# Attention outputs kept in each pattern's own order until the merge

## The chip, the cores and the metric

One Trainium2 chip, one core of it. The metric is the device time of one execution in microseconds. The profile names the engines PE (matrix multiply; PEld is its loading of weights), DVE (vector), ACT (scalar), POOL (GpSimd) and SP, whose queue issues the DMAs.

## The reference

A trunk of two layers on one sequence of 1024 tokens, width 1024: a gated mixer and an MLP, then an attention mixer and an MLP. The change concerns the attention mixer alone. It has 16 heads of 64 and three dilation patterns. Each pattern has its own queries, keys and values; a token sees only tokens of its own residue class modulo the dilation, in blocks of up to 128 with the block before. The outputs of the three patterns are weighted by a softmax over their log-sums:

```python
B_PATTERNS = ((128, 1), (512, 4), (2048, 16))

def mixer_b(h, w_qkv, w_out, slopes):
    qkv = (h @ w_qkv).reshape(B, S, N_PAT, 3, B_HEADS, B_HEAD_DIM)
    for g, (window, dilation) in enumerate(B_PATTERNS):
        o, lse = dilated_branch(qkv[:, :, g, 0], qkv[:, :, g, 1], qkv[:, :, g, 2], window, dilation, slopes)
        outs.append(o)
        lses.append(lse)
    wts = jax.nn.softmax(jnp.stack(lses, axis=0), axis=0)[..., None]
    o = jnp.sum(wts * jnp.stack(outs, axis=0), axis=0)
    return o.reshape(B, S, B_HEADS * B_HEAD_DIM).astype(h.dtype) @ w_out
```

## The kernel before, in words

All matrices are float32. A product is made of three passes, high by high, high by low and low by high part; `split` (L102 and L103) makes the two parts, the high one by a copy on ACT, the low one by a subtraction on DVE.

The attention stage works on pairs of heads, `hp` 0 to 7, and for each pair on the patterns `g` in the order 2, 1, 0: 24 groups. While the projections of later groups run on PE (`project`, L1139, with the splits of q and k and the copy of v), the softmax of the present group runs between them. The groups are cut into 8 slots of three positions, and `at(slot, pos)` puts a step into one of them: `scores` (L1212, L1213; on DVE L1219, on ACT the exponential L1221), `transposes` of the weights p (L1244, L1247, then a split into pThi and pTlo) and `weighted`, the products with v (L1267). This gives an order in the program. When the program is built, the framework's planner orders the instructions of each engine after its own model of their times, and each engine then works strictly in that order, waiting where something is not ready. The same holds for the DMAs on SP's queue.

Queries, keys and values of patterns 1 and 2 lie in the pattern's order, all tokens of one residue class side by side: in pattern 1 position `r * 256 + i` is token `4 * i + r`, in pattern 2 position `(a * 2 + b) * 64 + i` is token `16 * i + 8 * b + a`. `project` brings them into that order as it reads PSUM (`by_pos`, `perm`).

`weighted` sums the products of one head and pattern in two PSUM banks `pvs`, 512 tokens each. The high and the low part of v give two sums in the two halves of the partitions, `rest` and `main`. When both banks are full, ACT copies the one half into the tile `oT` (L1284) and DVE adds the other (L1285), 64 partitions by 512 elements each, for `b` in 0 and 1. `oT` holds both heads of the pair, 128 partitions by 1024 tokens; it is a tile of the pool `work`, tag "res", which has three buffers, one for each pattern. The residual rows of the output stage (`add_x`, L283 and L284) later use the same three buffers. In patterns 1 and 2 the destination is written in token order, so with a step of 4 or of 16 elements.

`merge` follows each pair. `statistics`, `read` and `factors` bring the sums and maxima of the three patterns through memory into token order and make the weights; `spread` reads them back, spread over 64 partitions for each head, into three tiles `bc` (`row_bc`: pool `vec`, tag "lng", three buffers; L1349). `scale` (L1352) multiplies oT by bc, pattern 1 on POOL, patterns 2 and 0 on DVE, and `add` (L1355) adds the three on DVE. For pairs 0 to 6 the sum goes to `o_dram` (L1357).

The output stage begins within the last group: `prepare` reads the sums of the pairs back into `oraw` (L1400; the first four are `row_bc` tiles, the others use the tag "raw" of the weights) and splits them into `oTs`; the last pair's sum is taken from the tile itself. `OutRows` loads the rows of the output matrix (L339, `wo_raw`), multiplies them by the gate on POOL (L344), splits them and multiplies (L356); ACT copies the first sums out (L374), DVE adds the later ones (L376).

## Time and profile before

| | |
|---|---|
| median of 3 runs | 2809.95 us (2809.93 to 2812.29) |
| profiled execution | 2810.59 us, of it the span 2808.9 us |
| attention stage | about 1040 to 2150 us |
| one pair of heads | about 133 us |

The first section of the page gives the busy time of each engine with its share of the span. In the rows of groups, the name left of the arrow is the tile written, right of it the tiles read, then the shapes, the count and the busy time with the mean of one in ns. In rows in order of time the columns are the start, the duration (both us), engine, line, operation and tiles; in brackets stands how long the engine had been idle and what ended that. In answers for one line the three numbers are the shortest, median and longest duration in ns. In rows of waits they are the sum in us, how many, and the longest.

### The profile page before, as it was taken

The numbers are of one execution on the slowest core, as the hardware profiler recorded it, in microseconds if no ns is written. First come the engines' busy times: TensorE is split into PE (matmuls) and PEld (weight loads), VectorE is DVE, ScalarE is ACT, GpSimd is POOL, SyncE is SP. The second block draws the span as 40 slices with busy tenths as digits, with TensorE's granted clock in tenths as the row PEclk, the third lists the DMA queues.
The fourth block names the chain that finished last, engine by engine and source line by source line (L and its number), as shares of the span: only waits on it lengthen the run. The fifth ranks groups of instructions, "written<-read, shape, count | busy, mean of one in ns | idle before, by whom it ended". The sixth has DMA issues, their size and how long they took to land.

```text
span 2808.9 us, 36869 instructions
## 1 busy us (share of the span) xinstructions
PE 2743.5 (98%) x13290; PEld 2279.7 (81%) x13290; DVE 1949.5 (69%) x3502; ACT 1418.3 (50%) x2625; POOL 200.7 (7%) x155
## 2 busy tenths in 40 slices
PE   6999999999999999999999999999999999999998
PEld 5787878888888878888888888888877788878887
DVE  6777798887977665556555555555659975668887
ACT  3354375555443455555555555555563755554332
POOL 1001000000000033101000000010201000000000
PEclk9999999999999999999999999999999999999999
DMA  7543347668846443212121212121215464486562
GB/s 256 159 127 105 120 152 234 214 225 280 281 152 196 133 150 111 57 47 65 37 68 39 69 32 69 39 69 38 85 47 172 164 215 150 161 285 207 168 199 93
DMA packets 300187, 384.15 MB, mean 137 GB/s; under 512 B 47533, under 2 KB 172885, under 8 KB 300005
## 3 DMA queue, kind: packets, MB, share of 16 engines
q1 hardware_dynamic: 300004, 381.80, 42.6%
q8 instruction: 104, 1.70, 0.3%
q14 instruction: 79, 0.64, 0.1%
HBM read 297.77 MB, written 83.97 MB: 136 GB/s over the span
## 4 chain that ended last, share of the span: by engine, by line
PE 77%; DVE 10%; DMA 7%; ACT 3%; issue 2%; POOL 1%; SPq 1%; DVEq 0%; POOLq 0%; ACTq 0%
PE psd L938 21%; PE psq L1139 8%; PE psv L1139 8%; PE psua L779 8%; PE psk L1139 7%; PE psuc L779 4%; PE psd_wout L356 3%; PE pv L1267 2%; DMA adaw<-in_ada_w_dram 2%; PE psu L356 2%; PE psd_wo L356 2%; PE psub L779 2%; PE psv L453 2%; PE sc L1213 1%; PE pT L1244 1%
## 5 line engine op out<-in xcount | busy, mean ns | idle before, releaser
L779 PE MATMUL psua<-right,left 128*128 128x512 f32 x1536 | 365.2, 391 | 3.3 <-ACT right L102 1.7
L938 PE MATMUL psd<-rhi,lhi 128*128 128x512 f32 x896 | 350.0, 391 | 3.0 <-ACT part L810 3.0
L938 PE MATMUL psd<-rlo,lhi 128*128 128x512 f32 x896 | 349.8, 390 | 0.2
L938 PE MATMUL psd<-rhi,llo 128*128 128x512 f32 x896 | 349.3, 390 | 0.0
L779 PEld LDWEIGHTS psua<-right,left 128*128 128x128 f32 x1536 | 287.2, 188 | 65.0 <-DVE right L103 2.9
L1221 ACT ACTIVATE p<-p,stat 128x128 f32<-128x128 f32 (+1 forms) x384 | 170.2, 444 | 231.6 <-DVE stat L1219 230.7
L1139 PE MATMUL psv<-hT,wv_hi 128*128 128x512 f32 x768 | 245.9, 401 | 2.4 <-DVE qlo L103 2.4
L1139 PE MATMUL psq<-hT,wq_hi 128*128 128x512 f32 x768 | 248.1, 404 | 0.0
L1139 PE MATMUL psk<-hT,wk_hi 128*128 128x512 f32 x768 | 247.2, 403 | 0.0
L103 DVE TENSOR_TENSOR pTlo<-pT,pThi 128x512 fp32r<-128x512 f32 (+1 forms) x160 | 98.0, 621 | 158.2 <-ACT pThi L102 157.3
L938 PEld LDWEIGHTS psd<-rhi,lhi 128*128 128x128 f32 x896 | 168.7, 188 | 38.9 <-ACT part L810 3.9
L938 PEld LDWEIGHTS psd<-rlo,lhi 128*128 128x128 f32 x896 | 168.5, 188 | 35.8 <-DVE rlo L103 1.1
L938 PEld LDWEIGHTS psd<-rhi,llo 128*128 128x128 f32 x896 | 168.7, 188 | 35.0
L779 PE MATMUL psuc<-right,left 128*128 128x512 f32 x768 | 190.5, 395 | 0.0
L128 DVE SCALAR_TENSOR_TENSOR adaacc<-adaw,silu_c,adaacc 128x512 f32<-128x512 f32 x168 | 132.7, 800 | 57.9 <-DMA adaw<-in_ada_w_dram 57.3
L779 PEld LDWEIGHTS psuc<-right,left 128*128 128x128 f32 x768 | 145.6, 191 | 30.9 <-DVE right L103 0.4
L1285 DVE TENSOR_TENSOR oT<-oT,pv 64x512 f32<-64x512 f32 x96 | 90.8, 946 | 109.3 <-ACT oT L1284 108.6
L1139 PE MATMUL psq<-hT,wq_lo 128*128 128x512 f32 x384 | 151.4, 394 | 0.0
L1139 PEld LDWEIGHTS psv<-hT,wv_hi 128*128 128x128 f32 x768 | 133.2, 189 | 22.1 <-issue 2.8
L1139 PE MATMUL psv<-hT,wv_lo 128*128 128x512 f32 x384 | 150.8, 393 | 0.0
L1139 PE MATMUL psk<-hT,wk_lo 128*128 128x512 f32 x384 | 150.6, 392 | 0.0
L1139 PEld LDWEIGHTS psk<-hT,wk_hi 128*128 128x128 f32 x768 | 133.7, 190 | 19.6
(250 smaller groups left out, 5841.2 us busy)
## 6 DMA issues: line engine op xcount, KB each, us to landing
lraw<-forms SPq DMA_DIRECT2D x112, 512.0 KB
adaw<-in_ada_w_dram SPq DMA_DIRECT2D x192, 256.0 KB
up<-in_mlp_w_up_dram SPq DMA_DIRECT2D x64, 512.0 KB
forms<-s SPq DMA_DIRECT2D x128, 256.0 KB
rraw<-in_mlp_w_down_dram SPq DMA_DIRECT2D x64, 512.0 KB
forms<-part SPq DMA_DIRECT2D x96, 256.0 KB
spill<-acc SPq DMA_DIRECT2D x24, 512.0 KB
wq_raw<-in_b_w_qkv_dram SPq DMA_DIRECT2D x24, 512.0 KB
```

Of the source, the lines that this page charges most:

```text
L103: return first, lo_engine.tensor_tensor(lo, src, hi, op=ALU.subtract)
L128: ins = V.scalar_tensor_tensor(acc[:], raw[:], silu_c[:, k : k + 1], acc[:], ALU.mult, ALU.add)
L356: T.matmul(dst, s[a], m[b], start=(n == 0), stop=(n == last))
L453: T.matmul(sums[u, half][:], units[u][a_][:, k * P : (k + 1) * P], hT[half][b_][:, k, :], start=k == 0 and a_ + b_ == 0, stop=k == KD - 1 ...
L779: T.matmul(acc, w[:, a, k, :], right[p][:, b, k, :], start=p in (1, 2, 5) and k + a + b == 0, stop=k == 3 and a == 1, skip_group_check=True)
L938: ins = T.matmul(sums[kind, m][:], l[a][:, k, m * P : (m + 1) * P], r[b][:, k, :], start=p in (1, 5, 2, 3) and kp + k + a + b == 0, stop=k ...
L1139: T.matmul(p[:], wu[a][:, k * P : (k + 1) * P], hT[half][b][:, k, :], start=k + c_ == 0, stop=k == KD - 1 and c_ == 2)
L1213: T.matmul(scb[:, sl], my["qlo"][e][:, tq], keys[:, k0 : k0 + w], start=False, stop=True)
L1221: A.activation(pr[:, 0:w], pr[:, 0:w], AF.Exp, bias=nm, scale=-1.0, accum_out=l)
L1244: T.transpose(pst[:, o : o + P], probs[t][:, P : 2 * P] if has[t] else probs[t][:, 0:P], ident[:])
L1267: T.matmul(pvs[b][:, q0 % HALF : q0 % HALF + w_], stt, x_[:, o_ : o_ + w_], start=not begun[b], stop=left[b] == 0, skip_group_check=True)
L1285: V.tensor_tensor(dst, dst, sb, op=ALU.add)
```

## The change

The sums of patterns 1 and 2 are written to oT in the pattern's own order, as those of pattern 0 always were: contiguous pieces of 512. The scale now reads oT with a step, in token order, and writes its product into the weights' tile bc, which is in token order. The adds work on the bc tiles, the store to o_dram reads the bc tile of pattern 0, and the last pair's sum is that tile. So oT is last used by its scale, and the three bc tiles are held until the adds and the store are done.

```diff
-                            if g == 0:
-                                dst = oT[rows, b * HALF : (b + 1) * HALF]
-                                sa, sb = pvs[b][rest, :], pvs[b][main, :]
-                            elif g == 1:
-                                dst = by_pos(oT[rows, :], g)[:, 2 * b : 2 * b + 2, :]
-                                sa, sb = (pvs[b][r, :].rearrange("p (r i) -> p r i", r=2) for r in (rest, main))
-                            else:
-                                dst = by_pos(oT[rows, :], g)[:, 4 * b : 4 * b + 4, :, :]
-                                sa, sb = (pvs[b][r, :].rearrange("p (a b i) -> p a b i", a=4, b=2) for r in (rest, main))
-                            A.copy(dst, sa)
-                            V.tensor_tensor(dst, dst, sb, op=ALU.add)
+                            dst = oT[rows, b * HALF : (b + 1) * HALF]
+                            A.copy(dst, pvs[b][rest, :])
+                            V.tensor_tensor(dst, dst, pvs[b][main, :], op=ALU.add)
...
                 def scale(g, engine):
-                    engine.tensor_tensor(oTs[g][:], oTs[g][:], box[g][:], op=ALU.mult)
+
+                    o, bc = oTs[g][:], box[g][:]
+                    if g == 1:
+                        o, bc = o.rearrange("p (r i) -> p i r", r=4), bc.rearrange("p (i r) -> p i r", r=4)
+                    elif g == 2:
+                        o = o.rearrange("p (a b i) -> p i b a", a=8, b=2)
+                        bc = bc.rearrange("p (i b a) -> p i b a", a=8, b=2)
+                    engine.tensor_tensor(bc, o, bc, op=ALU.mult)
 
                 def add(g):
-                    V.tensor_tensor(oTs[0][:], oTs[0][:], oTs[g][:], op=ALU.add)
-                    if g == 2 and hp < N_PAIRS - 1:
-                        nc.sync.dma_start(o_dram[hp], oTs[0][:])
+                    V.tensor_tensor(box[0][:], box[0][:], box[g][:], op=ALU.add)
+                    if g == 2:
+                        if hp < N_PAIRS - 1:
+                            nc.sync.dma_start(o_dram[hp], box[0][:])
+                        else:
+                            oTs["sum"] = box[0]
...
                     if k == N_PAIRS - 1:
-                        raw = oTs[0]
+                        raw = oTs["sum"]
```

## The prediction

> **What bounds the kernel now.** I read the page first, then the busy time by stretches, then who PE waited for in the attention stage, and last the order of time around each merge.

> ```profile
> span 2808.9 us, 36869 instructions
> ...
> PE 2743.5 (98%) x13290; PEld 2279.7 (81%) x13290; DVE 1949.5 (69%) x3502; ACT 1418.3 (50%) x2625; POOL 200.7 (7%) x155
> ...
> PE 77%; DVE 10%; DMA 7%; ACT 3%; issue 2%; POOL 1%; SPq 1%; DVEq 0%; POOLq 0%; ACTq 0%
> ```

> PE carries the span. The change touches only the attention stage, which lies between 1040 and 2150 us. Its busy times, with the columns PE, PEld, DVE, ACT, POOL, granted clock, DMA share and GB/s:

> ```profile
> core 0: us, PE busy (x) PEld busy (x) DVE busy (x) ACT busy (x) POOL busy (x), PEclk, DMA share, GB/s
> 1183.00:1316.00 133.00, 132.90 (x724) 112.93 (x723) 75.34 (x185) 72.84 (x175) 13.17 (x13) 1.00 0.20 53
> 2120.00:2142.00 22.00, 16.83 (x54) 12.13 (x55) 21.02 (x26) 4.42 (x5) 2.38 (x1) 0.84 0.69 224
> ```

> One pair of heads takes 133 us. In it PE is busy 132.90 us and DVE and ACT a little over half. Work taken from DVE or ACT there is worth nothing unless PE waits for exactly that work. Behind the last pair the picture is turned round: DVE is busy 21.02 of 22 us and PE only 16.83. There DVE sets the pace. What PE waited for in the two places:

> ```profile
> PEld pT L1244 <- ACT p L1221: 5.1, 13, 1.1
> PE psd_wo L356 <- DVE acc L376: 3.8, 2, 2.0
> ```

> So all waits of PE's loads for the softmax weights sum to 5.1 us in the whole stage, and they stand mostly at the merges, which the change edits. The third merge, in order of time:

> ```profile
> 1452.15 2.40 POOL L1352 TENSOR_TENSOR oT<-oT,bc 128x1024 f32<-128x1024 f32 x1 [1.73 <-DMA bc<-w_dram]
> 1454.29 1.35 DVE L1352 TENSOR_TENSOR oT<-oT,bc 128x1024 f32<-128x1024 f32 x1 [0.55 <-DMA bc<-w_dram]
> 1456.61 0.29 DVE L1219 CUSTOM_DVE_ANT_0 p<-sc,bias 128x128 f32<-128x128 f32 x1
> 1457.18 0.39 ACT L1221 ACTIVATE p<-p,stat 128x128 f32<-128x128 f32 x1
> 1457.71 0.14 PEld L1244 LDWEIGHTS pT<-ident,p 128*128 128x128 f32 x1 [0.24 <-ACT p L1221]
> ```

> POOL scales pattern 1 (L1352), DVE scales pattern 2 (also L1352), and only behind that on DVE stand the scores p (L1219), which ACT exponentiates and PE transposes. PE is already waiting 0.24 us for it. The chain weights, scale, p, exp, transpose has no slack: whatever lengthens the scale on DVE stops PE for as long.

> **The change: the copies become cheap.** L1284 and L1285 write patterns 1 and 2 (4 of the 6 write pairs of each head) with a step now; afterwards all are like pattern 0.

> ```profile
> L1284 ACT COPY oT<-pv x96: 565/1041/1091, 1051.6 to 2095.3; 64x512 f32<-64x512 f32 x96
> 1440.35 0.69 DVE L1285 TENSOR_TENSOR oT<-oT,pv 64x512 f32<-64x512 f32 x1 [0.81 <-ACT oT L1284]
> 1462.29 1.05 DVE L1285 TENSOR_TENSOR oT<-oT,pv 64x512 f32<-64x512 f32 x1
> 1095.54 1.12 DVE L1285 TENSOR_TENSOR oT<-oT,pv 64x512 f32<-64x512 f32 x1 [1.86 <-ACT oT L1284]
> L103 DVE TENSOR_TENSOR qlo<-psq,q 64x512 fp32r<-64x512 f32 x13 | 8.9, 688 | 4.0 <-ACT q L102 3.7
> ```

> The rows at 1440, 1462 and 1095 are patterns 0, 2 and 1. DVE saves 0.36 to 0.43 us on each of 64 adds, ACT 1041 - 565 = 0.48 us on each of 64 copies, together some 25 and 30 us of busy time. PE hides nearly all of it. I find one place where PE waits behind such an add:

> ```profile
> 1999.62 1.03 DVE L1285 TENSOR_TENSOR oT<-oT,pv 64x512 f32<-64x512 f32 x1
> 2001.49 0.71 PE L1244 MATMUL pT<-ident,p 128*128 128x128 f32 x2 [0.52 <-ACT p L1221]
> ```

> Two stepped adds stand ahead of that p on DVE, 2 x 0.36 = 0.7 us, about what PE loses there with its load: -0.7 us.

> **The merge becomes dear.** Its instruction count stays (three scales, two adds, one store), but two scales now read oT with a step: pattern 1 on POOL with a step of 256 elements, pattern 2 on DVE with 128. The trace before has no read of SBUF with such a step alone. Bounds for DVE: nothing from below, since the qlo row reads PSUM with a step in two patterns of three and costs 688 ns like an unstepped add; from above ACT's stepped write, (1041 - 565)/512 = 0.93 ns an element, 0.95 us for 1024. A gain is excluded: no row of such an instruction in this stage, stepped or not, is shorter than the unstepped one. I take the stepped L1285, the same engine and instruction and the nearest row, whose first input is also read with a step: 1.05 - 0.69 = 0.36 us for 512 elements, 0.72 us for 1024. Bounds for POOL: nothing, if its 2.34 ns an element cover it, to the same 0.95; I take 0.82, between pattern 2 (0.72) and pattern 1 on DVE (1.12 - 0.69 = 0.43 us for 512, 0.86), since it reads pattern 1 but at its own pace.

> [...]

> POOL's price reaches DVE, because DVE's scale does not run while POOL's does. Five merges, POOL and DVE (third merge above):

> ```profile
> 1185.64 2.40 POOL L1352 TENSOR_TENSOR oT<-oT,bc 128x1024 f32<-128x1024 f32 x1 [1.30 <-DMA bc<-w_dram]
> 1188.45 1.23 DVE L1352 TENSOR_TENSOR oT<-oT,bc 128x1024 f32<-128x1024 f32 x1 [0.55 <-DMA bc<-w_dram]
> 1318.77 2.40 POOL L1352 TENSOR_TENSOR oT<-oT,bc 128x1024 f32<-128x1024 f32 x1 [1.28 <-DMA bc<-w_dram]
> 1321.10 1.23 DVE L1352 TENSOR_TENSOR oT<-oT,bc 128x1024 f32<-128x1024 f32 x1
> 1585.07 2.40 POOL L1352 TENSOR_TENSOR oT<-oT,bc 128x1024 f32<-128x1024 f32 x1 [1.62 <-DMA bc<-w_dram]
> 1587.07 1.48 DVE L1352 TENSOR_TENSOR oT<-oT,bc 128x1024 f32<-128x1024 f32 x1
> 1984.82 2.40 POOL L1352 TENSOR_TENSOR oT<-oT,bc 128x1024 f32<-128x1024 f32 x1 [1.32 <-DMA bc<-w_dram]
> 1986.96 1.34 DVE L1352 TENSOR_TENSOR oT<-oT,bc 128x1024 f32<-128x1024 f32 x1 [0.77 <-DMA bc<-w_dram]
> ```

> Where they overlap, DVE ends 1.08 us after POOL each time: 1455.64 - 1454.55, 1588.55 - 1587.47, 1988.30 - 1987.22. So the new end is POOL's end + 0.82 + 1.08 + 0.72. First merge: 1190.66 against 1189.68, +0.98 (POOL had 0.41 us of room). Second: 1323.79 against 1322.33, +1.46. Third, fourth and seventh: +1.53, +1.54, +1.54. That the second has no slack for PE either shows here:

> ```profile
> 1323.88 0.39 ACT L1221 ACTIVATE p<-p,stat 128x128 f32<-128x128 f32 x1
> 1324.12 0.61 PE L1244 MATMUL pT<-ident,p 128*128 128x128 f32 x4
> ```

> The weight is ready at 1324.27 and its two transposes start in the second half of that group, just behind. The mean of the five is 1.41; for seven merges **+9.9 us**. Behind the scale the k split, p, the scale of pattern 0, the two adds and the split of the next pT move by the same amount, and PE with them, so they cost nothing more.

> **The eighth merge and what follows.**

> ```profile
> 2108.01 2.39 POOL L1352 TENSOR_TENSOR oT<-oT,bc 128x1024 f32<-128x1024 f32 x1 [36.63 <-DMA bc<-w_dram]
> 2108.57 2.91 DVE L103 TENSOR_TENSOR wo_lo<-wo_raw,wo_hi 128x1024 fp32r<-128x1024 f32 x1
> L1355 DVE TENSOR_TENSOR oT<-oT,oT x16: 1208/1226/3175, 1192.5 to 2119.8; 128x1024 f32<-128x1024 f32 x16
> SPq L283 <- DVE oT L1355: 8.6, 2, 7.3
> DVE acc L284 <- DMA res<-spill: 1.0, 2, 0.7
> ```

> Here POOL holds up a split of DVE instead (2.91 us, ending 2111.48, again 1.08 after POOL), and DVE runs without a gap from there. PE waits for DVE's acc and wo_lo, so both prices count in full: 0.82 + 0.72 = **+1.5 us**.

> The buffers' lifetimes move. oT is now free after its scale instead of after the adds and the store, so the loads of the residual rows (L283), which wait 8.6 us on SP for L1355, can go earlier; DVE waited only 1.0 us in all for what they bring, so I put down half, -0.5. In return the weights' buffers are held through adds and store. Three loads of oraw (L1400) reuse them at the seventh merge:

> ```profile
> 1987.25 3.81 SPq L1400 DMA_DIRECT2D oraw<-o_dram  x3
> 1995.41 0.32 SPq L1357 DMA_DIRECT2D o_dram<-oT  x1
> 2044.30 0.60 ACT L102 CAST oTs<-oraw 128x512 fp32r<-128x512 f32 x1
> ```

> They were issued behind the scales and will wait for the adds and the store, that is until the store of 1995.41 (now 1.5 later) has landed: some 8 to 12 us later, and the next load on SP, wo_raw, with them. oraw is first split by ACT at 2044.30, so some 45 us hide this; without that cover it would be those 8 to 12 us. Earlier pairs reuse these buffers only 133 us later: 0.

> Sum: 9.9 + 1.5 - 0.7 - 0.5 = **+10.2 us**. The profiled execution took 2810.59 us (span 2808.9 and 1.7 around it), so 2820.8 on its own scale; it lies 0.64 above the median 2809.95, so I name **2820.2 us**.

> **Rivals.** *One price only.* If POOL's loop covers the step, each merge and the end pay 0.72: 8 x 0.72 - 1.2 = +4.6, 2814.6. If DVE reads for free and POOL does not, the same five merges give 0.26, 0.74 and three times 0.82, seven times the mean 0.69 is 4.8, and with 0.8 and -1.2 it is +4.4, 2814.4. For it: POOL takes twice DVE's time for the same unstepped scale (2.40 against 1.23), so its pace is set by something that may hide a step. Against: ACT and DVE, also of different pace, pay alike for stepped writes. Chance 0.23.

> *Stepped reads are free on both* (not slower). All of L1285's extra is then its write, as ACT's extra is, and the qlo row speaks for it. The merges cost what they did and -0.7 - 0.5 remain: 2808.8. It decides from a joint price below some 0.15 us a merge. Chance 0.16.

> *POOL pays far more.* Its inner row is only 4 elements long; if it handles rows one by one, say twice 2.40 us, each merge gets 1.58 more than forecast, 8 x 1.58 = 12.6: 2832.8. No POOL instruction before has short rows, so nothing speaks against it but POOL's even 2.40. Chance 0.08.

> *The planner orders DVE otherwise at the merges or the end*, so that k and p stand ahead of the scale: most of the 9.9 falls away. Against: the number and kind of instructions it places are the same. Chance 0.03.

> **The numbers.** The forecast has 0.50. The two upper prices, 0.95 each, would add 8 x (0.13 + 0.23) = 2.9: 2823.1. At the end a collision of POOL and DVE costs up to 3.17 - 1.22 = 1.95 us and may come or go, with PE's clock at 0.84 there: 2 to 3 us either way. So the range goes from 2808.8 - 2.8 = 2806 to 2823.1 + 2.9 = 2826 us, leaving out the far POOL price and the edges. About 0.2%, 5.6 us, is what a measurement of this kernel tells from no change. Faster: 0.05 of the free case, where the end goes better than the 2 to 3 us say, and the planner's 0.03, 0.08 in all. Same: 0.11 of the free case, 0.17 of one price only and 0.03 of the forecast, 0.31. Slower: 0.47, 0.06 and POOL's 0.08, 0.61.

> **What would show it.** L1284 and L1285 all at 0.58 and 0.69. POOL's L1352 at 3.2, half of DVE's at 1.95 or more where POOL overlaps it. PE waiting for p in each merge about 1.4 us longer than before. It is wrong if L1352 stays at 2.40 and 1.22, if POOL passes 4 us, or if p no longer follows the scale on DVE.

## The result, and the profile after

The changed kernel takes 2847.23 us (median of four runs, 2843.12 to 2850.64) against 2809.94: a ratio of 1.013, 95% interval 1.0112 to 1.0148. It is 37 us slower where 10 were forecast. The profiled execution took 2844.86 us, its span is 34.2 us longer than before's. From the page of the changed kernel, its span and busy times:

```profile
span 2843.1 us, 36871 instructions
...
PE 2754.5 (97%) x13290; PEld 2289.6 (81%) x13290; DVE 1930.3 (68%) x3502; ACT 1387.7 (49%) x2625; POOL 209.2 (7%) x155
```

The instructions on PE, DVE, ACT and POOL are as many as before. DVE has 19 us less to do, ACT 31 us less, and the kernel is slower: the copies became cheap and nobody was waiting for them. Where the time went is read from POOL's scales of the first, seventh and eighth merge, in order of time:

```profile
1187.72 2.91 POOL L1351 TENSOR_TENSOR bc<-oT,bc 128x1024 f32<-128x1024 f32 x1 [1.74 <-DMA bc<-w_dram]
2016.64 2.91 POOL L1351 TENSOR_TENSOR bc<-oT,bc 128x1024 f32<-128x1024 f32 x1 [1.49 <-DMA bc<-w_dram]
2143.88 2.96 POOL L1351 TENSOR_TENSOR bc<-oT,bc 128x1024 f32<-128x1024 f32 x1 [37.06 <-issue]
```

From the first to the seventh a pair takes (2016.64 - 1187.72) / 6 = 138.15 us; before, (1984.82 - 1185.64) / 6 = 133.20. That is 4.95 us a merge, 29.7 for six. The first scale starts 2.1 later, the stretch from the seventh to the eighth is 4.1 longer, and from the eighth to the end it is 699.2 instead of 700.9: together the 34.2. So 33.8 of it lie between the first scale and the eighth, with the merges. (The start of the first scale differs by some us among the kernels of this document, 1182.9 to 1189.9; why is open.) PE's waits for p, and the answer for the line of the scale (with who waited for it) and of the copy and the add:

```profile
PEld pT L1244 <- ACT p L1221: 26.3, 15, 4.0
PE pT L1244 <- ACT p L1221: 22.6, 8, 3.8
...
L1351 DVE TENSOR_TENSOR bc<-oT,bc x16: 1217/1561/2001, 1192.7 to 2151.6; 128x1024 f32<-128x1024 f32 x16
L1351 POOL TENSOR_TENSOR bc<-oT,bc x8: 2903/2924/2957, 1187.7 to 2143.9; 128x1024 f32<-128x1024 f32 x8
  ACT oT L1276: 24.2, 7
L1276 ACT COPY oT<-pv x96: 567/580/587, 1053.1 to 2131.3; 64x512 f32<-64x512 f32 x96
L1277 DVE TENSOR_TENSOR oT<-oT,pv x96: 674/686/692, 1053.7 to 2131.9; 64x512 f32<-64x512 f32 x96
```

The operations cost about what was said: copies 0.58, adds 0.69, POOL 2.92 (3.2 was said). But PE's loads wait 26.3 us for the softmax weights instead of 5.1, and there is a row that no one had forecast: ACT's copy of a sum waits for POOL's scale, at seven merges, 24.2 us. The third merge of the changed kernel in order of time, POOL, ACT, DVE and the end of PE's wait:

```profile
1463.28 2.92 POOL L1351 TENSOR_TENSOR bc<-oT,bc 128x1024 f32<-128x1024 f32 x1 [1.58 <-DMA bc<-w_dram]
1466.23 0.58 ACT L1276 COPY oT<-pv 64x512 f32<-64x512 f32 x1 [3.62 <-POOL bc L1351]
1466.84 0.58 ACT L102 CAST k<-psk 64x512 fp32r<-64x512 f32 x1
1466.84 0.68 DVE L1277 TENSOR_TENSOR oT<-oT,pv 64x512 f32<-64x512 f32 x1 [5.00 <-ACT oT L1276]
1467.55 0.68 DVE L103 TENSOR_TENSOR k<-psk,k 64x512 fp32r<-64x512 f32 x1
1468.27 1.91 DVE L1351 TENSOR_TENSOR bc<-oT,bc 128x1024 f32<-128x1024 f32 x1
1470.21 0.69 DVE L103 TENSOR_TENSOR k<-psk,k 64x512 fp32r<-64x512 f32 x1
1470.93 0.29 DVE L1219 CUSTOM_DVE_ANT_0 p<-sc,bias 128x128 f32<-128x128 f32 x1
1471.32 0.40 ACT L1221 ACTIVATE p<-p,stat 128x128 f32<-128x128 f32 x1 [2.47 <-DVE stat L1219]
1471.87 0.86 PE L1244 MATMUL pT<-ident,p 128*128 128x128 f32 x2 [3.29 <-ACT p L1221]
```

And the same merge before, the two rows that matter, beside those which the prediction shows:

```profile
1452.44 0.58 ACT L102 CAST k<-psk 64x512 fp32r<-64x512 f32 x1 [1.11 <-PE psk L1139]
...
1460.78 1.05 ACT L1284 COPY oT<-pv 64x512 f32<-64x512 f32 x1
```

Before, the cast of k ran while POOL was scaling (1452.44 beside 1452.15), and the first copy of the next pair's pattern 2 stood eight microseconds behind it, after the first add, and waited for nothing. Now the copy stands ahead of the cast. It writes an oT buffer, and the one it was given is free as soon as POOL has scaled it, not only after the adds. The planner therefore places the copy earlier, among the casts. On the chip POOL's scale begins late, at 1463.28 us here, since it waits for the weights to come back through memory, and ACT works in its order: the copy waits 3.62 us for POOL, the casts of k stand behind it, DVE sits idle for 5.00 us, and only then come the add, two splits, the stepped scale and the scores. PE stands still until 1471.87.

There is a second price. After each such wait PE comes back slowly. PE busy, other engines and granted clock in the 9 us from the third and from the fourth stall on, in the answer by stretches:

```profile
core 0: us, PE busy (x) PEld busy (x) DVE busy (x) ACT busy (x) POOL busy (x), PEclk, DMA share, GB/s
1468.31:1477.31 9.00, 5.71 (x19) 4.40 (x18) 8.06 (x12) 3.67 (x9) 1.31 (x1) 0.64 0.10 41
1607.25:1616.25 9.00, 5.98 (x26) 4.74 (x25) 8.05 (x16) 3.64 (x9) 1.31 (x1) 0.81 0.13 54
```

The starts of the projection's matmuls show it too. Two rows of PE, each a step of a half-clock run (the granted clock was 0.50 from 1470.82 to 1477.64 us):

```profile
1473.38 0.63 PE L1139 MATMUL psk<-hT,wk_lo 128*128 128x512 f32 x1
1473.81 1.05 PE L1139 MATMUL psk<-hT,wk_hi 128*128 128x512 f32 x2
```

1473.81 - 1473.38 = 0.43 us from one to the next, where they normally follow at 0.23. Counted over the seven merges, 54 such steps fill 24.3 us of the projection; at 0.24 each, the mean of such steps in the kernel before, that would be 13.0, so 11.3 us are lost. In the stretch from 1180 to 2105 us PE itself waits for p once at each merge:

```profile
PE pT L1244 <- ACT p L1221: 21.9, 7, 3.8
```

Before, the same row had 1.1 us, and no step in this stretch was at half clock. 21.9 - 1.1 + 11.3 = 32.1, nearly all of the 33.8.

### The profile page after: what moved, and what is told of

It is laid out like the page before. It is cut to its first block, busy times and chain, and to the rows that moved or that the text cites. A ratio compares the mean times of both kernels' runs of the same rounds, so it can differ in the third digit from the quotient of the medians.

```text
span 2843.1 us, 36871 instructions
## 1 busy us (share of the span) xinstructions
PE 2754.5 (97%) x13290; PEld 2289.6 (81%) x13290; DVE 1930.3 (68%) x3502; ACT 1387.7 (49%) x2625; POOL 209.2 (7%) x155
## 5 line engine op out<-in xcount | busy, mean ns | idle before, releaser
L1221 ACT ACTIVATE p<-p,stat 128x128 f32<-128x128 f32 (+1 forms) x384 | 170.2, 444 | 236.9 <-DVE stat L1219 236.2
L1139 PE MATMUL psk<-hT,wk_hi 128*128 128x512 f32 x768 | 253.3, 412 | 0.0
L103 DVE TENSOR_TENSOR pTlo<-pT,pThi 128x512 fp32r<-128x512 f32 (+1 forms) x160 | 98.0, 620 | 168.9 <-ACT pThi L102 167.9
L1219 DVE CUSTOM_DVE_ANT_0 p<-sc,bias 128x128 f32<-128x128 f32 (+1 forms) x384 | 119.3, 347 | 54.3 <-PE sc L1213 51.3
```

Source lines behind the costliest of these rows:

```text
L103: return first, lo_engine.tensor_tensor(lo, src, hi, op=ALU.subtract)
L1139: T.matmul(p[:], wu[a][:, k * P : (k + 1) * P], hT[half][b][:, k, :], start=k + c_ == 0, stop=k == KD - 1 and c_ == 2)
L1219: V.tensor_tensor_reduce(out=pr[:, 0:w], in0=scb[:, sl], in1=st["bias"][:, width - w :], scale=-0.125, scalar=3e38, op0=ALU.add, op1=ALU.m ...
L1221: A.activation(pr[:, 0:w], pr[:, 0:w], AF.Exp, bias=nm, scale=-1.0, accum_out=l)
```

## The experiments

The theory formed from these rows is that of the order: the loss comes from ACT, where the copy takes the freed buffer, stands ahead of the casts and waits for POOL. Its rival is that of the price, the prediction's: the loss is what the stepped reads cost, and the rest follows them. The times of before on the same chips were 2811.09 us (first four kernels) and 2811.19 (last four). The time of one pair is worked out as above, from the first and the seventh scale of POOL.

**The buffers without the layout.** Against the kernel before: the copies write in token order as before and the scales read without a step, but the product goes into bc and oT is free early:

```diff
 def scale(g, engine):
-    engine.tensor_tensor(oTs[g][:], oTs[g][:], box[g][:], op=ALU.mult)
+    engine.tensor_tensor(box[g][:], oTs[g][:], box[g][:], op=ALU.mult)
 
 def add(g):
-    V.tensor_tensor(oTs[0][:], oTs[0][:], oTs[g][:], op=ALU.add)
...
+    V.tensor_tensor(box[0][:], box[0][:], box[g][:], op=ALU.add)
...
```

> The kernel before with the buffers of the change and nothing else: copies and adds still write oT with a step, the scales read it without one, their product goes into the weights' tile, the adds work there. Theory of the buffer: oT of pattern 1 is free after POOL's scale instead of after the add, so the planner puts the next pair's first copy ahead of two k casts on ACT, where it waits for POOL's scale; the copy then costs 1.04 us and the add behind it 1.05. Each of seven merges loses 2.5 to 4 us and some more to a lower clock: 2833 to 2845 us. Theory of the stepped read alone (the prediction's): no stepped read, so 2807 to 2812 us.

Measured: 2837.86 us, ratio 1.0095 (1.0076 to 1.0113). Copies, adds and scales are no longer than before; the waits of PE from 1180 to 2105 us and the third merge:

```profile
PE pT L1244 <- ACT p L1221: 19.1, 7, 3.4
...
1462.98 2.39 POOL L1352 TENSOR_TENSOR bc<-oT,bc 128x1024 f32<-128x1024 f32 x1 [1.54 <-DMA bc<-w_dram]
1465.39 1.04 ACT L1284 COPY oT<-pv 64x512 f32<-64x512 f32 x1 [3.05 <-POOL bc L1352]
1466.46 0.58 ACT L102 CAST k<-psk 64x512 fp32r<-64x512 f32 x1
```

Same wait, same place, a pair takes 136.53 us. The buffers alone cost 27 us: the price of the reads can't be the main cause, since here there is none.

**The layout without the freed buffers.** In the changed kernel, after the adds a tiny DVE instruction reads one column of each oT, so that the buffers are held until then, as before:

```diff
...
 def add(g):
     V.tensor_tensor(box[0][:], box[0][:], box[g][:], op=ALU.add)
+    for q in ((1,) if g == 1 else (2, 0)):
+        V.tensor_tensor(box["hold"][:, q : q + 1], box[0][:, 0:1], oTs[q][:, 0:1], op=ALU.add)
```

> The changed kernel, but each add is followed by a tiny DVE addition (128x1) that reads the sum and the oT just used, so that oT is released after the adds as in the kernel before; three of them a pair, under 0.1 us each. Stepped reads stay. Theory of the buffer: the copy stands behind the k casts again and only the prices of the stepped reads are left, POOL 2.92 for 2.40 and DVE 1.91 for 1.23, 0.8 to 1.3 us a merge: 2815 to 2821 us. Theory of the stepped read alone: nothing gained, 2840 to 2850 us.

Measured: 2827.59 us, 1.0058 (1.0038 to 1.0079), above what was expected. A pair takes 134.45 us, 1.25 more than before, and the copy no longer waits. What the stepped reads do stands alone here, in the same views as above and one row of PE at the output stage:

```profile
PE pT L1244 <- ACT p L1221: 8.1, 7, 1.9
...
1458.12 0.58 ACT L102 CAST k<-psk 64x512 fp32r<-64x512 f32 x1 [0.79 <-PE psk L1139]
1458.35 2.95 POOL L1352 TENSOR_TENSOR bc<-oT,bc 128x1024 f32<-128x1024 f32 x1 [1.92 <-DMA bc<-w_dram]
1460.44 2.63 DVE L1352 TENSOR_TENSOR bc<-oT,bc 128x1024 f32<-128x1024 f32 x1 [1.03 <-DMA bc<-w_dram]
...
2129.93 0.79 PE L356 MATMUL psd_wo<-wo_hi,oTs 128*128 128x512 f32 x1 [15.57 <-ACT acc L374]
```

The merges do what the price alone gives (+1.25 each). The miss is at the two ends. The first scale starts 3.4 us later than before, and the time from the eighth scale to the end is 6.2 us longer: there PE waits 15.57 us for a copy on ACT that stands behind the split of the last pair's sum. Here both oT and bc are held through the eighth merge, which neither kernel does; that this holding is the cause is read from the trace, not tried.

**The copy later.** The changed kernel, with the copies and adds of the first head of pattern 2 one slot later and the first copy kept from being moved:

```diff
+            first = A.copy(dst, pvs[b][rest, :])
+            if g == 2 and e + b == 0:
+                tc.keep_in_program_order(first)
...
+    if g == 2 and e == 0:
+        at(base + 5, 1)(copies)
+    else:
+        copies()
```

> The changed kernel with the copies and adds of the first head of pattern 2 one slot later, the first copy kept in program order on ACT, so that it stands behind the k casts by the time POOL's scale has ended; all buffers as in the change. Theory of the buffer: the wait on ACT is gone, the stepped reads stay: 2813 to 2820 us. If the loss were the stepped reads' or the held weights' buffers': 2840 to 2850 us.

Measured: 2817.29 us, 1.0019 (1.0008 to 1.003); a pair takes 134.36 us. One edit in the order takes back 30 of the 37 us, the layout and the buffers unchanged. PE waits from 1180 to 2105 us, and DVE's scale of pattern 2 in the third merge:

```profile
PE pT L1244 <- ACT p L1221: 7.8, 7, 2.1
...
1455.99 2.75 DVE L1359 TENSOR_TENSOR bc<-oT,bc 128x1024 f32<-128x1024 f32 x1 [0.36 <-DMA bc<-w_dram]
```

POOL's scale started at 1453.99 and took 2.94, to 1456.93; DVE's ends at 1458.74, 1.81 later, where the prediction had 1.08 + 0.72. This is the case that it priced.

**The copy later and DVE's merge later.** In addition the DVE scales and the adds of pairs 0 to 6 stand in later slots, the scales kept from being moved, so that DVE neither meets POOL's scale nor delays the scores:

```diff
-    engine.tensor_tensor(bc, o, bc, op=ALU.mult)
+    ins = engine.tensor_tensor(bc, o, bc, op=ALU.mult)
+    if engine is V and hp < N_PAIRS - 1:
+        tc.keep_in_program_order(ins)
...
-    at(base + 2 + (n + 2) // 3, (n + 2) % 3)(f)
+    at(*((base + 2 + (n + 2) // 3, (n + 2) % 3) if n == 0 or hp == N_PAIRS - 1 else ((base + 5, 2), (base + 6, 0), (base + 6, 2), (base + 7, 0))[n - 1]))(f)
```

> As late, and for pairs 0 to 6 DVE's two scales and two adds stand in program order in later slots, so that k and p of the merge's slots come first; the change's buffers allow it, since POOL's scale alone frees the oT that the next pair needs first. Theory of the buffer and of the scale ahead of p: both waits are gone, PE waits for p nowhere at the merges, 2803 to 2810 us, at or below the kernel before. If the stepped reads cost more than their place ahead of p (a port held, a longer copy): over 2815 us.

Measured: 2803.76 us, 0.9975 (0.9965 to 0.9985): 0.25% under the kernel before, and 43 us under the changed one. The third merge:

```profile
1454.79 2.94 POOL L1359 TENSOR_TENSOR bc<-oT,bc 128x1024 f32<-128x1024 f32 x1 [1.87 <-DMA bc<-w_dram]
1455.50 0.69 DVE L103 TENSOR_TENSOR k<-psk,k 64x512 fp32r<-64x512 f32 x1 [2.44 <-ACT k L102]
1457.56 0.29 DVE L1219 CUSTOM_DVE_ANT_0 p<-sc,bias 128x128 f32<-128x128 f32 x1
1465.48 0.57 ACT L1259 COPY oT<-pv 64x512 f32<-64x512 f32 x1
1466.69 2.00 DVE L1359 TENSOR_TENSOR bc<-oT,bc 128x1024 f32<-128x1024 f32 x1
```

The splits of k run beside POOL's scale, the scores follow at once, and the stepped scale of 2.00 us lies where PE has work. Among PE's waits from 1180 to 2105 us the row of L1244 and p is gone; a pair takes 132.79 us.

**The changed order without the step.** The changed kernel with scales that read straight on; this leaves out bringing patterns 1 and 2 into token order:

> The changed kernel with the scales reading oT without a step, so that patterns 1 and 2 are weighted in the wrong token order (that part of the computation is changed); copies, buffers and the planner's order are the change's. Theory of the buffer: the copy still stands ahead of the k casts and waits for POOL's scale, now 2.40 us instead of 2.92, and DVE's scale is 1.22 instead of 1.91, so each of seven merges is 1.2 us shorter than in the changed kernel and still 3 to 3.5 longer than before: 20 to 27 us over the kernel before. Theory of the stepped read alone: nothing stepped is left, at or below the kernel before.

Measured: 2829.07 us, 1.0063 (1.0047 to 1.0078), 17.9 us over the kernel before and so a little under what was expected. A pair takes 136.80 us, 3.60 more than before and just over the 3 to 3.5 that were expected; but the first scale starts 2.8 us earlier than before and the end is 1.5 shorter. The waits of PE, and the copy in the third merge:

```profile
PE pT L1244 <- ACT p L1221: 14.5, 7, 2.5
...
1459.25 0.59 ACT L1276 COPY oT<-pv 64x512 f32<-64x512 f32 x1 [3.17 <-POOL bc L1351]
```

With the held buffers this closes a square of four. Against 133.20 us for a pair before: the step alone +1.25, the freed buffers alone +3.60, both +4.95. The two add up (4.85), and the buffers are three quarters of it. Two things blur the square a little. The kernel before has stepped copies and the other three have not; freed buffers with stepped copies, the first experiment, cost 3.33. And these figures include what the half clock costs, which follows each of the seven merges with the freed buffers in both kernels, but only the seventh with the held ones.

**Only DVE's merge later**, the copy where the change has it:

> The changed kernel with DVE's two scales and two adds of pairs 0 to 6 in program order in later slots, as in late_spread, but with the early copy left where the planner puts it. Two waits in a row made the loss: ACT's copy behind POOL's scale, and DVE's stepped scale ahead of p. Only the second is gone here. Theory of the buffer: PE still waits for p behind copy, k cast and k split, 1 to 2 us a merge: 7 to 16 us over the kernel before. If DVE's scale ahead of p were all of it: at or below the kernel before, like late_spread.

Measured: 2833.53 us, 1.0085 (1.0068 to 1.0102), above what was expected. A pair takes 136.73 us. Taking DVE's scale out of the way helps little (138.15 before it) while the copy still waits:

```profile
PE pT L1244 <- ACT p L1221: 13.5, 7, 2.6
...
1459.69 0.58 ACT L1276 COPY oT<-pv 64x512 f32<-64x512 f32 x1 [3.67 <-POOL bc L1351]
1464.02 0.86 PE L1244 MATMUL pT<-ident,p 128*128 128x128 f32 x2 [2.59 <-ACT p L1221]
```

What was missed in the expectation is the clock: the waits sum to 13.5 us only, but every one of the seven is followed by a half-clock run (18.4 us of such steps in the projection, 8.6 of them lost).

**Is the layout worth anything?** The best kernel with the stepped copies and the unstepped scales of before, and the best kernel once more beside it:

> late_spread with the layout of the kernel before: copies and adds write oT with a step, the scales read it without one; buffers and order are those of late_spread. If the gain of late_spread comes from order and buffers alone, this one is as fast, within 0.2%, since PE hides the longer copies. If the cheaper copies and adds are worth anything by themselves, it is slower than late_spread by up to the 55 us of busy time that they save, in practice some 2 to 6 us.

> late_spread once more, beside late_spread_old on one chip: 0.2 to 0.35% below the kernel before, as in its first run.

Measured: 2808.10 us, 0.9989 (0.9978 to 1.0), and 2805.28 us, 0.998 (0.9971 to 0.999). A pair takes 133.21 and 132.72 us. So some 0.5 us a pair may be gained from the layout once nothing waits for the merge, but the intervals overlap: that the layout itself is worth 0.1% is likely and not settled. Most of what the best kernel has over the changed one is order.

## Why the prediction was wrong

- *The copies become cheap*: L1276 and L1277 at 0.58 and 0.69 us, as said, and worth next to nothing, as said.
- *The merge becomes dear*: POOL pays 0.52 us (2.92 against 2.40) where 0.82 was put down, DVE 0.67 to 0.77 (1.90 to 2.00 against 1.23) where 0.72 was. 2.92 / 2.40 is 22% more, with one of the two inputs read with a step. With the held buffers a merge cost 1.25 us against the 1.41 forecast. This term came out right, 7 x 1.25 = 8.8 us of 9.9, though POOL's part of it was put 0.30 us too high.
- *"Behind the scale ... move by the same amount ... cost nothing more"*: this failed through the clock. Each of the seven waits of the changed kernel brought a half-clock run, 11.3 us in all; where the price stood alone, with the held buffers, one of seven did.
- *The buffers' lifetimes*: here the prediction broke. It said that "oT is now free after its scale" and followed this only to the residual loads at the end; of reuse by earlier pairs it spoke for the weights' buffers alone, "Earlier pairs reuse these buffers only 133 us later: 0". The oT buffers are reused within microseconds, by the next pair's first copy on ACT. That step was left out, and it is 3.60 us a merge (measured without the step in the reads), 25 in all.
- *The planner orders DVE otherwise*, a rival with a chance of 0.03, argued away because "the number and kind of instructions it places are the same". The number was; the moment at which a buffer is free was not. It was ACT that came in another order, not DVE, and for the worse. That the planner goes by the release is read from the orders: with the buffers held until the adds, the copy stands behind the casts again.
- *The end*: forecast +1.0 with the residual loads, measured -1.7 from the eighth scale on. The residual loads (first two rows, SP's waits) now wait for the scales, 8.7 us in all where it was 8.6. The first load of oraw (third row) moved from 2.4 us behind POOL's scale of the seventh merge to 2027.33 - 2016.64 = 10.7, which is 8.3 later and within the 8 to 12 forecast; ACT splits it at 2080.8, so it remained hidden.

```profile
SPq L283 <- DVE bc L1351: 4.7, 2, 2.6
SPq L283 <- POOL bc L1351: 4.0, 1, 4.0
...
2027.33 0.34 SPq L1402 DMA_DIRECT2D oraw<-o_dram  x1
L102 ACT CAST oTs<-oraw x14: 602/621/632, 2080.8 to 2155.2; 128x512 fp32r<-128x512 f32 x14
```

The direction was right and the range ended 21 us too low (2826 against the median of 2847), nearly all from the one step left out and the half clock that it brings.

## What to carry to other kernels

A change of which buffer holds a result is a change of when the next writer may start; list that next writer, its engine and what is queued behind it, before costing the instructions. An instruction that an order puts early because its buffer is free on paper makes its whole engine wait if the release comes late on the chip: here ACT waited 24.2 us in seven such copies. Where PE is the bound, a wait can cost more than its length: here 11.3 us were lost in the steps behind 21.9 us of PE's waits. Look at the granted clock just behind it.

## What the runs showed of the hardware

```profile
1190.92:1194.34 3.42, 2.07 (x11) 1.47 (x9) 2.99 (x3) 1.49 (x3) 0.00 (x0) 1.00 0.56 147
1194.34:1197.75 3.41, 1.39 (x6) 1.07 (x7) 3.31 (x8) 1.47 (x5) 1.31 (x1) 1.00 0.01 2
1197.75:1201.16 3.41, 3.41 (x11) 2.83 (x10) 3.35 (x7) 1.85 (x3) 0.00 (x0) 0.50 0.07 28
...
1193.41:1196.82 3.41, 2.04 (x11) 1.44 (x9) 3.32 (x4) 1.11 (x2) 0.00 (x0) 1.00 0.40 114
1196.82:1200.23 3.41, 2.09 (x11) 1.66 (x11) 3.35 (x8) 1.72 (x6) 1.31 (x1) 1.00 0.01 2
...
1597.50:1600.91 3.41, 1.60 (x9) 0.96 (x8) 1.89 (x6) 1.46 (x5) 0.40 (x1) 1.00 0.16 47
```

  The next two rows, from the kernel with the buffers alone, hold one stall, 1.37 + 1.32 = 2.69 us of idle PE (60% and 61%), and no half clock followed; the last, from the kernel with only DVE's merge later, holds 1.81 us of idle PE (47%), and a half clock followed. So what went with a half clock here is how little PE was busy in one such stretch, not the length of the stall. No run moved a stall against these points, so this is read from the traces and not tried.
- DVE's scale hardly advanced while POOL's ran: it took 2.63 and 2.75 us where the stepped ones met, 1.91 and 2.00 where they didn't; without a step 1.35 and 1.48 against 1.23. The splits of k, which read PSUM and SBUF, ran beside it at 0.69.
- A step cost time in a write of ACT and in reads of DVE and POOL. ACT's write with a step of 4 or 16 elements cost 1.04 instead of 0.58 us for 512 elements. DVE's read with a step of 128 elements cost about 0.7 us more for 1024, POOL's with a step of 256 0.52 more.
